# Gathering the first expert's tokens alone, and moving the buffers that its routing uses, in a two-layer flow backbone

## The chip, the cores and the metric

One core of a Trainium2 chip runs the whole program in one launch. The metric is the device time of that core in microseconds (us), from the profiler's clock, as the median over runs.

## What is computed

Two layers. Each layer has a token mixer (four parallel branches, merged and projected by `w_out`) and then a mixture of 16 experts with expert choice: each expert takes its 32 best tokens of a stream. There are two streams of 256 tokens (context and latent); the second layer's experts work on the latent one alone. Cut to what matters here:

```python
def expert_choice_moe(h, router, w1, w3, w2):
    cap = CAPACITY_FACTOR * L // N_EXPERTS                      # 32
    aff = jax.nn.softmax((h @ router).astype(jnp.float32), axis=-1)
    g, idx = lax.top_k(aff.transpose(0, 2, 1), cap)
    xg = jax.vmap(lambda hb, ib: hb[ib])(h, idx)                # (B, 16, 32, 1024)
    a = jnp.einsum('becd,edf->becf', xg, w1)
    b = jnp.einsum('becd,edf->becf', xg, w3)
    y = jnp.einsum('becf,efd->becd', jax.nn.silu(a) * b, w2) * g[..., None]
    return scatter_add(zeros, idx, y)                           # (B, 256, 1024)

def layer(xx):
    xx = xx + mod_x[2] * token_mixer(modulate(xx, norm1_g, ...))
    hx = modulate(xx, norm2_g, mod_x[3], mod_x[4])
    return xx + mod_x[5] * expert_choice_moe(hx, moe_router, moe_w1, moe_w3, moe_w2)
```

All arithmetic is in float32. The weights of the experts are 16 x 3 x 4 MB in each layer.

## The kernel before

SBUF is cut by hand into columns: a base region, a left region (`rb`) and a right region (`rm`, 12288 columns). In a mixer, `rm` holds the hi/lo split of the projections' input; during an MoE, all that is free becomes slots for weights.

**The order of the work.** One program builds all layers, and a scheduling layer orders the instructions of each engine; the code's order is its guide. All weight loads stand in one queue, SP's, which issues in order: a DMA whose slot is still being read holds up those behind it.

**Before an MoE.** `MoePre` (L632 to L674) prepares the routing while the mixer's last projection `w_out` (called `wo` here) runs: the router's weights times the modulation (`AR`), the squares of x (`sq`) and the token sums and logits (`TokenSums`, L573 to L615). It takes the buffer `xt` (x with tokens on partitions) from the end of the base region. `transposes` (L666) fills `xt` by 128x128 transposes on PE and copies on ACT (L674).

**The MoE** (`moe`, L1435). Logits are scaled, softmax runs (exp on ACT at L1454), affinities are transposed, and four rounds of max, max_index and match_replace on DVE (L1468 to L1472) give each expert's 32 tokens; L1473 casts their indices. Then:

- `one_hot(gr)` (L1569) makes the selection matrix `OH` of group `gr` (four experts, 128 columns): a product on DVE (L1571), a broadcast by a matmul with ones, and a comparison with the token numbers on DVE (L1577).
- `gather(gr)` (L1580) multiplies `xt` (the stationary operand, 128x128) by `OH`: 8 chunks k of 128 features, for each stream and each half of the tokens one matmul instruction with 128 moving columns: 32 instructions in the first MoE, 16 in the second. A float32 instruction shows as two records in the trace. The results are scaled and shifted on their way out of PSUM, by ACT (L1605) and DVE (L1603) in turn.
- `weights` (L1607) takes 4 slots of 2048 columns (1 MB each) and issues their DMAs (L1614). An expert has 12 such tiles: 4 of `w1`, 4 of `w3`, 4 of `w2`.
- `ffn(e)` (L1618): 16 instructions for `w1`, 16 for `w3` (PSUM tag `pd`), SiLU on ACT (L1636), a product on DVE (L1637), four transposes (L1640), a copy (L1641), 16 instructions for `w2` (PSUM tag `ps`). A slot is free again when the four instructions that read its tile are through; `use` (L1504) passes it on, and for the first expert gives the first freed ones to buffers that were not there yet.

**The slots' order** (L1484 to L1500): first those of `rb`, then the free ones of the base region, then those of `rm`, last the columns where x itself lay (`xsl`). A slot in `rm` can't be filled before the mixer's last matmul that reads `rm`; one in the base region that covers `AR` and `sq` not before the token logits are done. In the main loop (L1728) group 0 is gathered whole, then the experts run in order; the next group is gathered after the third expert of the one before.

Of the kernel before, what the change touches and what calls it, by code (L numbers as in the profile page):

```python
# [13 lines left out]
AF = mybir.ActivationFunctionType  # L14
OP = mybir.AluOpType
AX = mybir.AxisListType

D = 1024
L = 256
KB = 8  # L20
NE = 16
CAP = 32
# [327 lines left out]
def view(b, off, n):  # L350
    return Buf(b.mem, b.at + off, n)


def build(tc, ins, outT, dbg=None, stop=None):
    nc = tc.nc
    V, A, T, G, S = nc.vector, nc.scalar, nc.tensor, nc.gpsimd, nc.sync
    big = tc.tile_pool(name="big", bufs=1)
    pool = big.__enter__()
    mem = Mem(pool.tile([128, BASE], F32, name="base"), BASE, small=768)
# [17 lines left out]
    def ps(tag):  # L377
        cnt[0] += 1
        return pp.tile([128, 512], F32, name=f"p{tag}{cnt[0]}", tag=tag, bufs=BUFS[tag])
# [9 lines left out]
    mod = [mem.take(96) for _ in range(2)]  # L389
# [4 lines left out]
    ada_raws = [mem.take(512) for _ in range(2)]  # L394
# [14 lines left out]
    def cs(name, off=0, dims=None, **kw):  # L409
        o, c = CN.at[name]  # L410
        if dims is None:
            dims = [[1, kw.pop("n", c - off)]]
        return cn(o + off, dims, **kw)
# [13 lines left out]
    def tr(out, in_):  # L427
        T.transpose(out, in_, ident)  # L428

    def mm(out, lhsT, rhs, start, stop, **kw):  # L430
        return T.matmul(out, lhsT, rhs, start=start, stop=stop, **kw)  # L431
# [141 lines left out]
    class TokenSums:  # L573
# [24 lines left out]
        def tokens(self, mem):  # L598

            W, ns = 512 - self.t0, self.ns  # L600
            out = ps("m")
            part = [mem.take(W) for _ in range(2 if self.AR else 1)]
            V.tensor_copy(part[0](), self.p2[:, 0:W])
            if self.AR:
                A.activation(part[1](n=256), self.pr[:, 0:256], AF.Copy)
            for s in range(ns):
                for tb in range(2):
                    i, c = tb * ns + s, s * 256 + tb * 128
                    mm(out[:, i:i + 1], part[0](c, n=128), cs("one1"), True, True)
            for tb in range(2 if self.AR else 0):  # L610
                mm(out[:, 64 + tb * ns * 16:64 + (tb + 1) * ns * 16], part[1](tb * 128, n=128),
                   cs("ssum" if ns == 1 else "ssum2"), True, True)
            for b in part:
                b.free()
            return out  # L615

    def rs_tokens(p, ns, mem):
# [14 lines left out]
    class MoePre:  # L632


        def __init__(self, l, t0):
            self.l, self.t0 = l, t0
            self.nb = (512 - t0) // 128
            self.ns = self.nb // 2
            self.Ac = mod_cols(l, "g2", 4)
            mem.merge()  # L640
            n = self.nb * D
            self.xt = mem.take_at(mem.end - n, n)
            self.AR = mem.take(512)
            V.tensor_tensor(self.AR(0, [[64, 8], [32, 2], [1, 32]]), sp(l, "router", 0, [[32, 8], [0, 2], [1, 32]]),
                            self.Ac(0, [[2, 8], [1, 2], [0, 32]]), op=OP.mult)
            p = ps("m")
            for k in range(KB):
                mm(p[0:32, 0:2], sp(l, "router", k * 32, n=32), mod[l](3 * 16 + k * 2, n=2), k == 0, k == KB - 1)
            t = mem.take(2)
            V.tensor_copy(t(n=2, np_=32), p[0:32, 0:2])  # L650
            p = ps("m")
            for s in range(2):
                mm(p[:, s * 16:s * 16 + 16], t(s, [[0, 128]], np_=32), cs("ident", n=16, np_=32), True, True)
            t.free()
            self.shr = mem.take(32)
            V.tensor_copy(self.shr(n=32), p[:, 0:32])
            self.sq = [mem.take(512 - t0) for _ in range(4)]
            self.sums = TokenSums(t0, self.sq, self.AR)

        def step(self, k):  # L660
            self.sums.step(k)
            if k == KB - 1:
                for b in self.sq + [self.AR]:
                    b.free()

        def transposes(self):  # L666
            for kh in range(2):
                for i in range(self.nb):
                    p = ps("s")
                    s, tb = divmod(i, 2)  # L670
                    s += 2 - self.ns
                    for q in range(4):
                        tr(p[:, q * 128:q * 128 + 128], xb[0](s * 2048 - xb[1] + (kh * 4 + q) * 256 + tb * 128, n=128))
                    A.activation(self.xt(i * D + kh * 512, n=512), p, AF.Copy)  # L674
# [760 lines left out]
    def moe(l, last, rm, rb, pre, ahead):  # L1435
        t0 = 256 if last else 0
        W = 512 - t0
        NS = 1 if last else 2
        nt = NS * CAP
# [3 lines left out]
        n = nb * 16  # L1443
# [5 lines left out]
                        op=OP.mult)  # L1449
# [8 lines left out]
        ne = NS * 16  # L1458
# [4 lines left out]
        V.tensor_copy(at[0](np_=ne), pa[0:ne, 0:256])  # L1463
        gi = mem.take(64)
        iu = mem.take(32)
        pre.transposes()
        for r in range(4):
            g8, i8, rows = gi(32 + 8 * r, n=8, np_=ne), iu(8 * r, n=8, np_=ne).bitcast(U32), at[r](np_=ne)  # L1468
            V.max(g8, rows)
# [7 lines left out]
        ge = view(raws[2], 512, 256)  # L1477
        OH = view(raws[2], 0, W)
        xg = [view(raws[0], 0, KB * 4 * nt), None]
# [4 lines left out]
        slots = []  # L1484
        for m in (rb, mem, rm):
            m.merge()
            try:
                while True:
                    slots.append(m.take(2048))
            except MemoryError:  # L1490
                pass
            if m is mem:
                late = Buf(mem, cn.at + LATE, 2048)
                slots.append(late)

        x_at, nx = xb[0].at, xb[0].n
        xb[0].free()
# [68 lines left out]
                    else:  # L1566
                        A.activation(dst, src, AF.Copy)

        def one_hot(gr):  # L1569

            V.tensor_tensor(ge(0, [[128, NS], [32, 4], [1, 32]], np_=ne), gi(0, [[0, NS], [0, 4], [1, 32]], np_=ne),  # L1571
                            cs("sel", gr, [[4, NS], [8, 4], [0, 32]], np_=ne), op=OP.mult)
            p = ps("m")
            mm(p[:, 0:NS * 128], cs("ones", np_=ne), ge(n=NS * 128, np_=ne), True, True)
            for s in range(NS):
                for tb in range(2):
                    V.tensor_scalar(OH((s * 2 + tb) * 128, n=128), p[:, s * 128:s * 128 + 128], cs("tok", tb, n=1),  # L1577
                                    rs(8 + tb * NS + s, n=1), op0=OP.is_equal, op1=OP.mult)

        def gather(gr, j0=0, nj=4):  # L1580
            if j0 == 0:
                one_hot(gr)
            x = xg[gr % 2]
            n = nj * 32
            per = min(KB, 512 // (NS * n))
            for k0 in range(0, KB, per):
                p = ps("m")
                ks = range(k0, min(KB, k0 + per))
                for k in ks:
                    for s in range(NS):  # L1590
                        c = ((k - k0) * NS + s) * n
                        for tb in range(2):
                            mm(p[:, c:c + n], pre.xt((s * 2 + tb) * D + k * 128, n=128), OH((s * 2 + tb) * 128 + j0 * 32, n=n),
                               tb == 0, tb == 1)
                for k in ks:
                    for s in range(NS):
                        c = ((k - k0) * NS + s) * n
                        ci = k * 2 + s + 2 - NS
                        src = p[:, c:c + n].rearrange("p (j c) -> p j c", j=nj)
                        dst = x(k * 4 * nt + j0 * nt + s * CAP, [[nt, nj], [1, CAP]])  # L1600
                        A_, sh = pre.Ac(ci, n=1), mod[l](3 * 16 + ci, n=1)
                        if (k + s) % 2:
                            V.tensor_scalar(dst, src, A_, sh, op0=OP.mult, op1=OP.add)  # L1603
                        else:
                            A.activation(dst, src, AF.Identity, bias=sh, scale=A_)  # L1605
# [12 lines left out]
        def ffn(e):  # L1618
            gr, j = divmod(e, 4)
            x = xg[gr % 2]  # L1620
            w1, w3 = weights(0, e), weights(1, e)
            pa, pb = ps("d"), ps("d")
            for p, w in ((pa, w1), (pb, w3)):
                for k in range(KB):
                    for half in range(2):
                        mm(p[half * nt:half * nt + nt, :], x((k * 4 + j) * nt, n=nt),
                           w[k // 2]((k % 2) * 1024 + half * 512, n=512), k == 0, k == KB - 1)
            read = w1 + w3
            n0 = len(slots)
            for b in read[::-1] if e == 0 else read:  # L1630
# [3 lines left out]
            i = e % 2  # L1634
# [3 lines left out]
            p = ps("s")  # L1638
# [4 lines left out]
            if e == NE - 1:  # L1643
                src = ins["moe_w2"][l, e].rearrange("(k p) n -> p k n", p=128)
                c, o, pieces = 0, 2048, []
                for n in LASTW:
                    if o + KB * n > 2048:
                        b, o = slots.pop(0), 0
# [3 lines left out]
                    c, o = c + n, o + KB * n  # L1652
# [72 lines left out]
            S.dma_start(out=cn(LATE + n_, n=CN.n - LATE - n_), in_=ins["cn"][:, LATE + n_:])  # L1725

        nxt, spare = [], []
        gather(0)  # L1728
        for gr in range(4):
            for j in range(4):  # L1730
                ffn(4 * gr + j)
# [49 lines left out]
    for l in range(2):  # L1781
        with phase("right", F32R) as rm:
            if l == 0:
                ada = AdaBack([(0, c) for c in range(2, 5)], mem.take(2048))
            pre, ahead = mixer(l, l == 1, ada, rm, sums)
# [29 lines left out]
```

## Time and profile before

| | |
|---|---|
| runs | 2011.41, 2004.29, 2009.74 us; median 2009.74 |
| profiled execution | 2006.5 us; its span, first to last instruction, 2004.7 us |
| TensorE (PE) busy | 1843.2 us, 92% of the span |
| DVE, ACT, POOL busy | 854.7 (43%), 529.9 (26%), 27.9 (1%) us |
| expert weights | 382 DMAs of 1 MB on SP's queue, median 17 to 18 us from issue to landing |
| other large loads | 152 of 512 KB (`wg`), 96 of 512 KB (`ada_w`, `ada_t`) |

How to read it: PE is the matmul engine and PEld its weight loads, DVE the vector engine, ACT the scalar engine, SPq the queue of SyncE. The first MoE lies at about 645 to 1150 us, the second at about 1535 to 2000 us. A row of a timeline has its start, its length, the engine, the program's line and the operation, output<-input, and in brackets the idle time before and what ended it; "x32" merges 32 records of one kind, so that the length is that of all. A row of windows has, for a stretch, its length, the busy time of each engine (PE, PEld, DVE, ACT, POOL, records in brackets), the clock that PE was granted (1.00 is 2.4 GHz, 0.50 is 1.2 GHz), the DMA engines' share and GB/s.

### The profile page before, as it was taken

Reading aid. Unit: us, or ns where it says so; the run is one execution under the profiler, and the core shown is the slowest. Engines: PE = TensorE matmul, PEld = TensorE weight load, DVE = VectorE, ACT = ScalarE, POOL = GpSimd, SP = SyncE. Lnnn points to the kernel's source line nnn. Section 1 sums busy time; section 2 is a strip of 40 time slices with the busy share of each in tenths; the row PEclk is TensorE's granted clock in tenths of the full one; section 3 lists DMA queues with packets and bytes.
Section 4 is the critical chain, followed back from the end, with each engine's and each line's share of the span. In section 5 each row is a group of like instructions: output and inputs, shape, how many; then the busy total and the mean of one; then the engine's idle time right before and its main releaser. Section 6 shows DMA issues by size and latency. Waiting matters only on the chain.

```text
span 2004.7 us, 28151 instructions
## 1 busy us (share of the span) xinstructions
PE 1843.2 (92%) x11524; PEld 1087.6 (54%) x11524; DVE 854.7 (43%) x1855; ACT 529.9 (26%) x932; POOL 27.9 (1%) x52
## 2 busy tenths in 40 slices
PE   7999999999999899999897799999998999987877
PEld 3667778877887443434232356788997333221213
DVE  5355658798743222221121345869865021110101
ACT  4433447522233110101000243447443000000000
POOL 0000000000000000000000010010000000000000
PEclk9989999999999899999999999999998999999999
DMA  8641122364545999999999855333578999999999
GB/s 312 223 140 58 64 85 78 107 236 136 194 156 218 353 399 350 387 409 409 409 409 409 302 189 180 117 106 137 200 262 336 409 409 409 409 409 409 409 409 332
DMA packets 154148, 550.07 MB, mean 274 GB/s; under 512 B 11042, under 2 KB 22690, under 8 KB 153124
## 3 DMA queue, kind: packets, MB, share of 16 engines
q1 hardware_dynamic: 153444, 545.13, 71.7%
q0 software_dynamic: 576, 3.15, 0.5%
q8 instruction: 91, 1.49, 0.3%
q14 instruction: 37, 0.30, 0.0%
HBM read 545.08 MB, written 3.15 MB: 273 GB/s over the span
## 4 chain that ended last, share of the span: by engine, by line
PE 69%; DMA 19%; DVE 7%; issue 3%; ACT 3%; SPq 0%; DVEq 0%; ACTq 0%
PE pd L431 40%; PE ps L431 15%; DMA base<-moe_w 8%; PE pm L431 7%; DMA r<-moe_w 6%; PE pa L431 4%; DMA base<-ada_w 2%; PE pm L428 1%; DMA base<-wg 1%; DVE base L527 1%; DVE r L844 1%; ACT r L843 1%; PE ps L1640 1%; DMA base<-cb 0%; DVE r L1236 0%
## 5 line engine op out<-in xcount | busy, mean ns | idle before, releaser
L431 PE MATMUL pd<-r 128*128 128x256 f32 (+3 forms) x2976 | 574.4, 364 | 12.9 <-DMA r<-moe_w 6.5
L431 PEld LDWEIGHTS pd<-r 128*128 128x128 f32 (+2 forms) x2976 | 427.3, 184 | 131.4 <-issue 53.8
L431 PE MATMUL pd<-r,r 128*128 128x512 f32 (+3 forms) x1304 | 282.6, 433 | 13.4 <-DMA r<-moe_w 10.8
L431 PEld LDWEIGHTS pd<-r,r 128*128 128x128 f32 (+2 forms) x1304 | 161.8, 166 | 105.0 <-issue 54.8
L844 DVE TENSOR_TENSOR r<-base,r 128x1024 fp32r<-128x1024 f32 x136 | 165.9, 1222 | 110.4 <-ACT r L843 110.0
L843 ACT ACTIVATE r<-base 128x1024 fp32r<-128x1024 f32 x136 | 143.4, 1058 | 252.2 <-PE pd L431 181.2
L431 PE MATMUL ps<-base 32*64 32x64 f32 (+12 forms) x2372 | 177.2, 279 | 15.1 <-DMA base<-hy 5.1
L431 PE MATMUL pd<-r,base 128*32 128x512 f32 (+1 forms) x680 | 166.5, 598 | 11.3 <-DMA r<-moe_w 10.6
L431 PEld LDWEIGHTS ps<-base 32*64 32x64 f32 (+7 forms) x2372 | 112.6, 142 | 76.3 <-issue 42.7
L431 PE MATMUL pm<-base 128*128 128x128 f32 (+12 forms) x660 | 106.1, 327 | 17.5 <-DVE base L1571 5.8
L431 PE MATMUL ps<-r,base 128*64 128x512 f32 (+4 forms) x468 | 98.6, 525 | 12.9 <-DVE base L1641 6.3
L431 PE MATMUL pd<-base 128*32 128x512 f32 (+1 forms) x408 | 100.5, 595 | 6.4 <-DMA base<-moe_w 5.6
L431 PEld LDWEIGHTS pm<-base 128*128 128x128 f32 (+5 forms) x660 | 72.8, 180 | 60.9 <-issue 33.6
L431 PEld LDWEIGHTS pd<-r,base 128*32 128x32 f32 (+1 forms) x680 | 42.0, 122 | 111.2 <-issue 76.4
L1637 DVE TENSOR_TENSOR r<-base,pd 64x512 f32<-64x512 f32 x16 | 10.9, 679 | 214.3 <-PE pd L431 214.3
L1637 DVE TENSOR_TENSOR base<-base,pd 128x512 f32<-128x512 f32 x16 | 11.0, 688 | 190.1 <-PE pd L431 155.9
L1636 ACT ACTIVATE base<-pd 128x512 f32<-128x512 f32 (+1 forms) x32 | 19.0, 594 | 251.1 <-PE pd L431 251.1
L431 PE MATMUL pa<-r,r 128*128 128x512 f32 (+1 forms) x384 | 82.4, 342 | 1.1 <-DVE base L905 1.1
L1687 ACT ACTIVATE base<-ps 32x512 f32<-32x512 f32 (+2 forms) x28 | 14.7, 525 | 251.6 <-PE ps L431 247.2
L1687 ACT ACTIVATE r<-ps 32x512 f32<-32x512 f32 (+2 forms) x32 | 15.3, 480 | 246.2 <-PE ps L431 240.3
L431 PE MATMUL pd<-base,r 128*32 128x512 f32 (+1 forms) x296 | 71.3, 597 | 9.3 <-DMA base<-moe_w 9.3
L1685 DVE COPY r<-ps 32x512 f32<-32x512 f32 (+2 forms) x32 | 17.8, 555 | 123.3 <-ACT r L1687 123.2
(246 smaller groups left out, 1728.8 us busy)
## 6 DMA issues: line engine op xcount, KB each, us to landing
r<-moe_w SPq DMA_DIRECT2D x251, 1024.0 KB, 18.1
base<-moe_w SPq DMA_DIRECT2D x131, 1024.0 KB, 17.4
base<-wg SPq DMA_DIRECT2D x152, 512.0 KB, 3.6
base<-ada_w SPq DMA_DIRECT2D x60, 512.0 KB, 4.7
base<-ada_t SPq DMA_DIRECT2D x24, 512.0 KB, 3.3
r<-ada_w SPq DMA_DIRECT2D x12, 512.0 KB, 10.2
base<-xT SPq DMA_DIRECT2D x4, 1024.0 KB, 6.8
filters<-r SPq DMA_DIRECT2D x8, 256.0 KB, 4.0
```

Source lines behind the costliest of these rows:

```text
L428: T.transpose(out, in_, ident)
L431: return T.matmul(out, lhsT, rhs, start=start, stop=stop, **kw)
L527: V.tensor_tensor_reduce(self.junk() if s == 0 else b(), b(), self.cb(s * 1024, n=1024), 1.0, cs("adab", l * 48 + c * 8 + j, n=1), OP.mult ...
L843: A.activation(w[0](), raw(), AF.Copy)
L844: V.tensor_tensor(w[1](), raw(), F(w[0]()), op=OP.subtract)
L1636: A.activation(s_(np_=rows), pa[0:rows, :], AF.Silu)
L1637: V.tensor_tensor(h_(np_=rows), s_(np_=rows), pb[0:rows, :], op=OP.mult)
L1640: T.transpose(p[:, q * rows:q * rows + rows], h_(q * 128, n=128, np_=rows), cs("ident", n=rows, np_=rows))
L1685: V.tensor_copy(dst, src)
L1687: A.activation(dst, src, AF.Copy)
```

## The change

1. **The first expert's tokens are gathered alone** (`gather_one`): `one_hot` and the matmuls for 32 columns instead of 128, all in one PSUM bank, and four DVE instructions to take it out. The other three experts' tokens are gathered inside `ffn(0)`, between `w1`/`w3` and `w2`, with 96 columns.
2. **A dummy exp** of one column is put on ACT at step 1 of the token sums.
3. **`xt` moves** from the end of the base region to the start of `rm`. `sq` and the sums' parts move to `ada_raws` in part, and `AR` away from the base region's end.
4. **The slots are sorted** by when they come free (`when`): `rb`, free base columns (and, in the second MoE, `rm` from 4096 to 8192), base columns under `AR` and `sq`, the other `rm` slots, and the late one.

```diff
@@ class MoePre
-            n = self.nb * D
-            self.xt = mem.take_at(mem.end - n, n)
-            self.AR = mem.take(512)
+            end = (mem.end - self.nb * D, mem.end)
+            self.AR = mem.take(512, end)
...
-            self.sq = [mem.take(512 - t0) for _ in range(4)]
+            self.sq = [view(ada_raws[i // 2], 256 * (i % 2), 256) if t0 else ada_raws[i] if i < 2 else mem.take(512, end)
+                       for i in range(4)]
+            self.own = [self.AR] if t0 else self.sq[2:] + [self.AR]
...
         def step(self, k):
             self.sums.step(k)
+            if k == 1:
+                z = mem.take(8)
+                A.activation(z(n=1), self.sq[1](0, n=1), AF.Exp, scale=-1.0)
+                z.free()
...
-        def transposes(self):
+        def transposes(self, rm):
+
+            self.xt = rm.take_at(0, self.nb * D)
@@ moe, slots
+        spot = [(b.at, b.at + b.n) for b in pre.own]
+        def when(b):
+            if b is late:
+                return 4
+            if b.mem is rm:
+                return 1 if 2 * KB * W <= b.at < 8192 else 3
+            return 2 if b.mem is mem and any(b.at < o1 and o0 < b.at + 2048 for o0, o1 in spot) else b.mem is mem
+        slots.sort(key=when)
@@ moe, gathers
-        def one_hot(gr):
+        def one_hot(gr, j0, nj):
...
+        def gather_one(gr):
+
+            one_hot(gr, 0, 1)
+            x, p, n = xg[gr % 2], ps("m"), NS * CAP
+            for k in range(KB):
+                for s in range(NS):
+                    c = k * n + s * CAP
+                    for tb in range(2):
+                        mm(p[:, c:c + CAP], pre.xt((s * 2 + tb) * D + k * 128, n=128), OH((s * 2 + tb) * 128, n=CAP),
+                           tb == 0, tb == 1)
+            for k in range(0, KB, 4):
+                dst = x(k * 4 * nt, [[4 * nt, 4], [CAP, NS], [1, CAP]])
+                src = p[:, k * n:(k + 4) * n].rearrange("p (k s c) -> p k s c", s=NS, c=CAP)
+                cols = lambda b, o: b(o + k * 2 + 2 - NS, [[2, 4], [1, NS], [0, CAP]])
+                V.tensor_tensor(dst, src, cols(pre.Ac, 0), op=OP.mult)
+                V.tensor_tensor(dst, dst, cols(mod[l], 48), op=OP.add)
...
         def gather(gr, j0=0, nj=4):
-            if j0 == 0:
-                one_hot(gr)
+            one_hot(gr, j0, nj)
@@ ffn, after the matmuls of w1 and w3
+            if e == 0:
+                gather(0, 1, 3)
@@ main loop
-        gather(0)
+        gather_one(0)
```

The order of the instructions, where the prediction speaks of it. On **PE**, the first MoE's routing to the first expert's `w2`, before (`pm` and `ps` are PSUM tiles; L428 are transposes, `pm` with 128x128 the gather, `pd` the experts' `w1` and `w3`, L1640 the transposes ahead of `w2`, `ps` with 64x512 `w2`):

```order
L431 MATMUL pm_4965<-base 128x256
L431 MATMUL pm_4971<-base 128x128 x8
L431 MATMUL pm_4984<-base 128x128 x8
L431 MATMUL pd_5031<-r_4867,base 64x512
L431 MATMUL pm_4997<-base 128x128 x8
L431 MATMUL pm_5010<-base 128x128 x8
L431 MATMUL pd_5031<-r_4867,base 64x512 x15
L431 MATMUL pd_5032<-r_4867,base 64x512 x8
L431 MATMUL pd_5032<-base 64x512 x8
L431 MATMUL pd_5106<-base 64x512
L1640 MATMUL ps_5067<-base 128x128 x4
L431 MATMUL pd_5106<-base 64x512 x2
```

and in the changed kernel (its L1675 is L1640 before):

```order
L431 MATMUL pm_4966<-base 128x64
L431 MATMUL pm_4972<-base,r_4872 128x32 x32
L431 MATMUL pm_5052<-base 128x192
L431 MATMUL pd_5017<-r_4868,base 64x512 x16
L431 MATMUL pd_5018<-r_4868,base 64x512 x8
L431 MATMUL pd_5018<-base 64x512 x8
L431 MATMUL pm_5058<-base,r_4872 128x96 x8
L431 MATMUL pm_5071<-base,r_4872 128x96 x8
L1675 MATMUL ps_5112<-base 128x128 x3
L431 MATMUL pm_5084<-base,r_4872 128x96 x8
L1675 MATMUL ps_5112<-base 128x128
L431 MATMUL pm_5097<-base,r_4872 128x96 x8
```

One gather of 32 instructions has become two: 32 narrow ones ahead of `w1`, and 32 of 96 columns ahead of the first `w2` (`ps_5122`, 16 instructions, which follows). The second MoE has the same with 16 and 16.

On **SP**, the first MoE's first tiles, before (`r_4867` is `rb`, `r_4871` is `rm`; `r_4867` x6 in the last row is the first reuse):

```order
L1614 DMA r_4867<-moe_w 128x2x1024 x2
L1614 DMA base<-moe_w 128x2x1024
L1614 DMA r_4871<-moe_w 128x2x1024
L1614 DMA base<-moe_w 128x2x1024 x2
L1614 DMA r_4871<-moe_w 128x2x1024 x5
L1614 DMA base<-moe_w 128x2x1024 x2
L1614 DMA r_4867<-moe_w 128x2x1024 x6
```

and in the changed kernel (its L1647 is L1614 before, `r_4868` is `rb`, `r_4872` is `rm`):

```order
L1647 DMA r_4868<-moe_w 128x2x1024 x2
L1647 DMA base<-moe_w 128x2x1024 x4
L1647 DMA r_4872<-moe_w 128x2x1024
L1647 DMA base<-moe_w 128x2x1024
L1647 DMA r_4872<-moe_w 128x2x1024 x3
L1647 DMA base<-moe_w 128x2x1024 x2
L1647 DMA r_4868<-moe_w 128x2x1024 x6
```

Three more tiles of the base region stand ahead of the first tile of `rm`, and two fewer are in `rm`. From the first row on, it is 13 tiles until the first reuse in both.

## Rows read from the trace of the kernel before

**Rows 1.** Page of before, part 2: GB/s in 40 slices of 50.1 us.
```profile
GB/s 312 223 140 58 64 85 78 107 236 136 194 156 218 353 399 350 387 409 409 409 409 409 302 189 180 117 106 137 200 262 336 409 409 409 409 409 409 409 409 332
```
**Rows 2.** Windows (us, busy times, granted clock, DMA share, GB/s), first MoE's start.
```profile
660.00:665.00 5.00, 4.49 (x20) 4.16 (x20) 1.69 (x5) 0.28 (x1) 0.00 (x0) 0.50 1.03 409
665.00:670.00 5.00, 5.00 (x36) 4.07 (x35) 1.46 (x4) 1.59 (x5) 0.00 (x0) 0.94 0.89 356
670.00:675.00 5.00, 5.00 (x32) 2.72 (x32) 1.46 (x4) 3.08 (x5) 0.00 (x0) 1.00 0.10 16
```
**Rows 3.** DMA issues on SP, first MoE: two reuses (start us, us, engine, line).
```profile
673.60 0.37 SPq L1614 DMA_DIRECT2D r<-moe_w  x1
689.86 0.37 SPq L1614 DMA_DIRECT2D base<-moe_w  x1
```
**Rows 4.** One DMA into an empty queue (KB, us from issue to landing), issue at 642.19.
```profile
r<-moe_w SPq DMA_DIRECT2D x1, 1024.0 KB, 4.7
```
**Rows 5.** Waits of PE (total us, times, longest us), 690 to 977 us.
```profile
PE ps L1640 <- DVE base L1637: 5.1, 7, 0.9
```
**Rows 6.** Waits of PE, 977 to 1121 us (end of the first MoE).
```profile
PE pd L431 <- DMA r<-moe_w: 9.7, 14, 2.0
```
**Rows 7.** Timeline of ACT, first MoE's routing.
```profile
650.28 1.28 ACT L1454 ACT_TABLE_LOAD   x1
651.58 0.26 ACT L1454 ACTIVATE base<-base 128x64 f32<-128x64 f32 x1
```
**Rows 8.** Timeline of DVE, first MoE's one-hot.
```profile
658.66 0.41 DVE L1571 TENSOR_TENSOR base<-base 32x256 f32<-32x256 f32 x1
660.38 1.37 DVE L1577 TENSOR_SCALAR base<-pm,base 128x128 f32<-128x128 f32 x4 [1.31 <-PE pm L431]
```
**Rows 9.** Timeline of PE, first MoE: one-hot, gather, first expert.
```profile
660.85 6.09 PE L431 MATMUL pm<-base 128*128 128x128 f32 x32 [0.51 <-DVE base L1577]
667.87 3.84 PE L431 MATMUL pm<-base 128*128 128x128 f32 x32
671.64 3.65 PE L431 MATMUL pd<-r,base 128*64 128x512 f32 x16
687.92 4.46 PE L431 MATMUL ps<-base 128*64 128x512 f32 x20
```
**Rows 10.** Timeline of PEld (weight loads), the same gather.
```profile
660.85 5.90 PEld L431 LDWEIGHTS pm<-base 128*128 128x128 f32 x32 [1.23 <-DVE base L1577]
667.87 3.65 PEld L431 LDWEIGHTS pm<-base 128*128 128x128 f32 x32 [0.81 <-ACT base L1605]
```
**Rows 11.** Timeline of PE, matmuls with one moving column, full clock.
```profile
645.76 1.45 PE L431 MATMUL pm<-base 128*128 128x1 f32 x12
```
**Rows 12.** Timeline of DVE, two pieces of the gather's evacuation.
```profile
670.46 0.73 DVE L1603 TENSOR_SCALAR base<-pm,base 128x128 f32<-128x128 f32 x2 [2.26 <-ACT base L1605]
```
**Rows 13.** DMA issues on SP, second MoE: first after `wo`, two reuses.
```profile
1534.18 0.37 SPq L1614 DMA_DIRECT2D base<-moe_w  x1
1553.26 0.37 SPq L1614 DMA_DIRECT2D base<-moe_w  x1
1569.39 0.37 SPq L1614 DMA_DIRECT2D r<-moe_w  x1
```
**Rows 14.** The DMA issued at 1553.26: us from issue to landing, behind a queue.
```profile
base<-moe_w SPq DMA_DIRECT2D x1, 1024.0 KB, 7.5
```
**Rows 15.** Timeline of PE, second MoE: `wo`'s end, gather, experts 0 and on.
```profile
1528.79 1.72 PE L431 MATMUL pd<-r 128*128 128x256 f32 x13
1545.62 5.75 PE L431 MATMUL pm<-base 128*128 128x128 f32 x32 [0.51 <-DVE base L1577]
1551.31 8.78 PE L431 MATMUL pd<-base 128*32 128x512 f32 x40
1567.45 2.74 PE L431 MATMUL ps<-r 128*32 128x512 f32 x12
```
**Rows 16.** Windows by engine, the second mixer after its first projections.
```profile
1180.00:1500.00 320.00, 308.78 (x2775) 266.61 (x2774) 226.35 (x533) 154.11 (x287) 14.03 (x28) 1.00 0.48 167
```

More of the change, by code (lines that the diff above doesn't have):

```diff
@@ L601, in tokens @@
             out = ps("m")
-            part = [mem.take(W) for _ in range(2 if self.AR else 1)]
+            part = [view(b, 0, W) for b in ada_raws] if self.AR else [mem.take(W)]
             V.tensor_copy(part[0](), self.p2[:, 0:W])
@@ L612, in tokens @@
                    cs("ssum" if ns == 1 else "ssum2"), True, True)
-            for b in part:
-                b.free()
+            if not self.AR:
+                part[0].free()
             return out
@@ L661, in step @@
             self.sums.step(k)
+            if k == 1:
+                z = mem.take(8)
+                A.activation(z(n=1), self.sq[1](0, n=1), AF.Exp, scale=-1.0)
+                z.free()
             if k == KB - 1:
-                for b in self.sq + [self.AR]:
+                for b in self.own:
                     b.free()
-        def transposes(self):
+        def transposes(self, rm):
+            self.xt = rm.take_at(0, self.nb * D)
             for kh in range(2):
@@ L1465, in moe @@
         iu = mem.take(32)
-        pre.transposes()
+        pre.transposes(rm)
         for r in range(4):
@@ L1567, in restore_x @@
                         A.activation(dst, src, AF.Copy)
-        def one_hot(gr):
-            V.tensor_tensor(ge(0, [[128, NS], [32, 4], [1, 32]], np_=ne), gi(0, [[0, NS], [0, 4], [1, 32]], np_=ne),
-                            cs("sel", gr, [[4, NS], [8, 4], [0, 32]], np_=ne), op=OP.mult)
+        def one_hot(gr, j0, nj):
+            n = nj * 32
+            V.tensor_tensor(ge(0, [[n, NS], [32, nj], [1, 32]], np_=ne), gi(0, [[0, NS], [0, nj], [1, 32]], np_=ne),
+                            cs("sel", j0 * 8 + gr, [[4, NS], [8, nj], [0, 32]], np_=ne), op=OP.mult)
             p = ps("m")
-            mm(p[:, 0:NS * 128], cs("ones", np_=ne), ge(n=NS * 128, np_=ne), True, True)
+            mm(p[:, 0:NS * n], cs("ones", np_=ne), ge(n=NS * n, np_=ne), True, True)
             for s in range(NS):
                 for tb in range(2):
-                    V.tensor_scalar(OH((s * 2 + tb) * 128, n=128), p[:, s * 128:s * 128 + 128], cs("tok", tb, n=1),
+                    V.tensor_scalar(OH((s * 2 + tb) * 128 + j0 * 32, n=n), p[:, s * n:s * n + n], cs("tok", tb, n=1),
                                     rs(8 + tb * NS + s, n=1), op0=OP.is_equal, op1=OP.mult)
+        def gather_one(gr):
[13 more added lines that the diff above has]
+                V.tensor_tensor(dst, dst, cols(mod[l], 48), op=OP.add)
         def gather(gr, j0=0, nj=4):
-            if j0 == 0:
-                one_hot(gr)
+            one_hot(gr, j0, nj)
             x = xg[gr % 2]
```

## The prediction

> **What bounds the kernel now.** I read the page's slices first, then the windows of the two stretches in which an MoE starts, then PE's waits, and last the timelines of SP, PE, DVE and ACT there. The slices show 409 GB/s in slices 17 to 21 and 31 to 38 [rows 1]: there weights stream without a pause. At that rate a tile of 1 MB takes 1.049 MB / 409 GB/s = 2.56 us; into an empty queue it lands 4.7 us after its issue [rows 4].
>
> *First MoE.* By SP's order 21 tiles fit before a slot is used twice. They have landed by about 670 us, and in 670 to 675 us only 16 GB/s move [rows 2]: the queue is dry until the first expert's first four `w1` instructions free a slot at 673.60; the slots that `w2` frees follow from 689.86 on [rows 3]. From 690 to 977 us PE waits for DVE and ACT alone, never for a weight; the 7 waits ahead of the transposes cost 0.7 us each [rows 5]. From 977 us on it waits for tile after tile [rows 6]. So PE sets the pace first, and as SP's issues hang on PE's reads, a delay of PE before 830 us moves the stream that ends the MoE by as much. Three tiles landing earlier before 645 us help nobody here: the number of tiles before the first reuse is the same.
>
> *Second MoE.* The stream begins with the issue at 1534.18 [rows 13] and runs at 409 GB/s to the end [rows 1], so each us by which it runs earlier, without a later gap, counts.
>
> **The change, part by part.** The sum is made against the profiled execution, 2006.5 us, which stands 3.2 us under the median shown (2009.74).
>
> *Early exp.* The table load takes 1.28 us right ahead of exp [rows 7]. The dummy moves it into `wo`'s stretch, where ACT has idle time. Some 0.2 us of it lay beside the end of exp's input, so I take -1.1 us (bounds 0 and -1.3). The SiLU's table load is behind exp in both kernels.
>
> *One-hot.* From its product to the first gather record 2.19 us pass (658.66 to 660.85), with 0.41 us for the product and 1.37 / 4 = 0.34 us for a comparison [rows 8, 9]. A quarter of the columns shortens all three steps; the fixed part of each isn't shown. I take -0.9 us (bounds 0 and -1.4).
>
> *`gather_one`, first MoE.* It starts at 660.85 - 2.0 = 658.85. It has 64 records, as many as the old gather, only narrower. The old ones took 6.09 / 32 = 0.19 us at clock 0.50 and 3.84 / 32 = 0.12 us at full clock [rows 2, 9], and a record with one moving column also takes 1.45 / 12 = 0.12 us [rows 11]: at full clock width costs nothing below 128 columns. At half clock I have no narrow record; bounds are 0.12 and 0.24 us, and I take 0.19, since the weight loads themselves stood 5.90 / 32 = 0.18 us apart there and 3.65 / 32 = 0.11 us after [rows 10]. The clock came back 0.6 us into 665 to 670 us (mean 0.94) [rows 2], 4.7 us after the gather's start; I take the same here, 24 records: 24 x 0.19 + 40 x 0.12 = 9.4 us, to 668.2. Then, behind the last matmul, a DVE product and the first sum: by 0.37 us for a piece of 128x128 [rows 12], 0.85 us, so `w1` begins at 669.05. Before, it ran from 671.64, with one instruction (0.43 us) done earlier [rows 9], so from 671.2. Gain: **-2.2 us**, and the first reuse at 673.60 comes earlier by as much.
>
> The Trainium skill (page "TensorE: Matmul & The Clock Gate", section "LDWEIGHTS (loading the stationary operand)") gives a weight load as its columns divided by 1.2 in ns, 107 ns for 128 columns, and makes no difference by the clock. By it the 64 narrow records would take 6.8 us instead of 9.4, the first MoE would lose 2.5 us less and the second 2.1 us less, and the sum below would be +1.2 instead of +5.8. The row at half clock, 0.18 us per load, speaks against it.
>
> *The other three experts' gather, first MoE.* 32 instructions more, 64 records of 96 columns at full clock: 64 x 0.117 = +7.5 us of PE, all between `w3` and `w2`. Its cover is one of the idle waits ahead of the transposes, 0.7 to 0.9 us [rows 5]: -0.8. So `w2`, from 687.92 before [rows 9], and with it the slots it frees from 689.86 on, come later by 7.5 - 0.8 - 2.2 = **+4.5 us**. Queued behind these slots on SP are all later tiles, and nothing of PE's work is removed elsewhere: the lag lasts to 977 us and passes into the stream. Bounds: +1.5 (narrow records at 0.12 us throughout, one-hot at its best) and +8 (half clock throughout, no gain from exp).
>
> *Slots, second MoE.* By SP's order 22 tiles are loaded before the first reuse in both; 15 instead of 14 are issued before `wo` ends, and the first after it goes to `rm`, which waits for `wo`'s last matmul at 1528.79 + 1.72 = 1530.5 [rows 15] instead of the token logits. It is issued 3.7 us before the 1534.18 of today, and one tile fewer stands behind it. But the 22 tiles then end the earlier: the next slot, freed by `w1` at 1553.26, took 7.5 us to land behind a queue, to 1560.8 [rows 13, 14]; without one it lands at 1558.2, -2.6 us. There is no exp load to save here. The narrow gather has 32 records: from 1545.1, 24 x 0.19 + 8 x 0.12 = 5.5 us, with evacuation `w1` starts at 1551.5, against 1551.31 [rows 15]. The wide one adds 32 x 0.117 = 3.7 us, less 0.6 us of idle, so `w2` starts 3.3 us later than 1567.45 [rows 15], and the slot that it freed at 1569.39 [rows 13] is free at 1572.7. The tile in it lands at 1572.7 + 4.7 = 1577.4; before, six tiles behind 1560.8, at 1576.1. A gap opens that the earlier start can't close: **+1.3 us**, to the end of the kernel. Bounds: -3 (the gate at `w2` doesn't bind) and +3.
>
> *The second mixer.* Experts' last tiles lie in other regions, so `rm` and the scan's matmuls come in another order there. From 1180 to 1500 us PE is busy 308.8 of 320 us [rows 16]: at most 11.2 us can be gained, and the order alone doesn't say which way. I take 0, with -3 and +11 as bounds.
>
> *Other edits.* `sq`, `AR` and the sums' parts in other places and the sort itself cost nothing: same instructions, beside `wo`'s matmuls.
>
> Sum: 4.5 + 1.3 + 0 = +5.8, so 2012.3 for an execution like the profiled one, 2015.5 on the median's footing. Between the two I forecast **2014 us**, a difference of 0.2%. About 0.5% (10 us) is what a measurement of this kernel can tell from no change, so the class is "no difference".
>
> **The rivals.**
> - *The earlier starts decide.* If the slots that `w1` frees carry the stream over `w2`'s delay, the first MoE keeps -2.2 and the second gains 2.6: 2014 - 5.8 - 4.8 = 2003 us. For it: the dry queue at 670 to 675 us and the 7.5 us of queue [rows 2, 14]. Against it: from 690 us on PE itself is the pace, and it has more to do. Chance 0.2.
> - *The clock stays low.* If narrow matmuls don't bring the clock back from 0.50 while `gather_one` runs, 40 records cost 0.07 us more, +2.8, and 8 in the second MoE, +0.6: 2017 us. For it: PE is idle ahead of the gather in both. Against it: the old gather got the clock back within itself. Chance 0.1. The Trainium skill (same page, "Why this matters for your kernels") warns that thin matmuls let the clock swing; the trace of before has no long run of such narrow ones at that place to show it.
> - *Slower.* In the second mixer the scan's matmuls, moved ahead of projections, wait for DVE without cover. It decides once PE's idle time in a stretch like 1180 to 1500 us, now 11.2 us [rows 16], grows by 6 us or more; doubled, the kernel takes 2014 + 11 = 2025 us. For it: the moved order; against it: most projections still stand beside the scans. Chance 0.1.
> - *The change doesn't do what it says.* If the tokens of the first expert come no earlier (the one-hot's fixed parts and the evacuation eat the gain) and the later gather fills waits more than I think, nothing moves: 2010 us. Chance 0.15.
>
> **How the numbers follow.** My forecast has 0.45. Faster by over 0.5%, below 1999.7 us, is a third to a half of the first rival: 0.09. Slower, above 2019.8, is over half of the third, and tails of the second and of the bounds: 0.10. The rest, 0.81, lies within 0.5%. The range reaches from 2001 us (most of the first rival) to 2021 us (upper bounds of the first MoE); outside are the ends of the first and third rival.
>
> **What would show it.** Right: in the first MoE a narrow gather of 64 records in about 9.4 us, `w1` some 2 us earlier, `w2` some 4 us later than 687.9, a dry queue of 5 us or more before `w2`'s first slot, and the MoE's last tile 4 us later; in the second MoE the first tile after `wo` issued near 1530.5 on the old footing, and a short gap in the stream near 1573. Wrong: `w2` of the first expert earlier than before, no gap behind the tiles that `w1`'s slots bring, a gather at clock 0.50 to its end, or PE's idle time in the second mixer changed by more than 3 us.

## The result, and the profile after

The changed kernel takes **2025.28 us** (median of 4 runs, 2021.65 to 2029.5) against 2007.01 us of the kernel before on the same chip (4 runs, 2000.78 to 2011.41): a ratio of **1.0084**, 95% interval 1.0059 to 1.0110. The medians are 18.3 us apart, and the ratio stands for 17 us (12 to 22): the change is slower. I had forecast no difference, and the time lies above my range. The profiled execution of the changed kernel has a span of 2019.6 us, 14.9 us over that of before.

In the page of the changed kernel the slices show the same picture as [rows 1], with 409 GB/s in the same slices of the first MoE and from one slice later on in the second:

```profile
GB/s 309 219 154 55 64 78 79 138 237 125 188 188 301 211 390 389 400 409 409 409 409 409 260 164 190 115 85 157 199 275 319 361 409 409 409 409 409 409 409 332
```

The first MoE tells most. These are the first copy of the transposes on ACT (a fixed point at the end of `wo`), and then PE's one-hot, narrow gather, `w1` with `w3`'s first half, the first half of the other experts' gather, and `w2`; they answer to [rows 9]:

```profile
639.80 0.60 ACT L681 ACTIVATE r<-ps 128x512 f32<-128x512 f32 x1 [0.88 <-PE ps L428]
651.87 0.68 PE L431 MATMUL pm<-base 32*128 32x64 f32 x2 [5.64 <-DVE base L1588]
652.96 13.86 PE L431 MATMUL pm<-base,r 128*128 128x32 f32 x64 [0.40 <-DVE base L1594]
668.00 12.30 PE L431 MATMUL pd<-r,base 128*64 128x512 f32 x48 [0.24 <-DVE base L1612]
683.66 3.81 PE L431 MATMUL pm<-base,r 128*128 128x96 f32 x32
692.56 7.09 PE L431 MATMUL ps<-base 128*64 128x512 f32 x32
```

The narrow gather took 13.86 us for 64 records, 0.217 us each, where I had 9.4 us. The windows (as in [rows 2]: length, busy times, granted clock, DMA share, GB/s) show why:

```profile
655.00:660.00 5.00, 5.00 (x25) 5.00 (x25) 0.00 (x0) 0.00 (x0) 0.00 (x0) 0.50 0.27 102
660.00:665.00 5.00, 5.00 (x25) 5.00 (x25) 0.00 (x0) 0.00 (x0) 0.00 (x0) 0.50 0.00 0
665.00:670.00 5.00, 4.76 (x17) 2.94 (x18) 2.89 (x9) 0.00 (x0) 0.00 (x0) 0.50 0.00 0
670.00:675.00 5.00, 5.00 (x22) 1.46 (x20) 0.00 (x0) 0.00 (x0) 0.00 (x0) 0.84 0.41 132
```

PE was busy without a pause, and its clock stayed at 0.50 (1.2 GHz) through the whole gather and into `w1`; `w1`, with the full clock in 670 to 675 us for part of the time, took 12.30 us for 48 records (0.256 us each, against 10.09 / 45 = 0.224 before, shown below). From 660 to 670 us no weight moved. SP's two reuses answer to [rows 3]:

```profile
671.72 0.37 SPq L1647 DMA_DIRECT2D r<-moe_w  x1
694.54 0.37 SPq L1647 DMA_DIRECT2D base<-moe_w  x1
```

ACT's first copy and `w1` in the first MoE before, and ACT's first copy in the second MoE, before and in the change:

```profile
645.52 0.60 ACT L674 ACTIVATE base<-ps 128x512 f32<-128x512 f32 x1 [1.06 <-PE ps L428]
671.64 10.09 PE L431 MATMUL pd<-r,base 128*64 128x512 f32 x45
1533.04 0.60 ACT L674 ACTIVATE base<-ps 128x512 f32<-128x512 f32 x1 [0.92 <-PE ps L428]
1540.24 0.60 ACT L681 ACTIVATE r<-ps 128x512 f32<-128x512 f32 x1 [0.83 <-PE ps L428]
```

From ACT's first copy to `w2` it was 692.56 - 639.80 = **52.8 us**. Before, that copy began at 645.52 and `w2` at 687.92 [rows 9]: 42.4 us. So `w2` came 10.4 us later (I had 4.5).

The second MoE, PE's narrow gather, `w1` and `w3`, second gather, `w2` (against [rows 15]), and two windows:

```profile
1552.67 7.03 PE L431 MATMUL pm<-base,r 128*128 128x32 f32 x32 [0.41 <-DVE base L1594]
1560.48 11.46 PE L431 MATMUL pd<-base 128*32 128x512 f32 x40
1577.02 3.81 PE L431 MATMUL pm<-base,r 128*128 128x96 f32 x32
1582.04 0.62 PE L431 MATMUL ps<-r 128*32 128x512 f32 x1
```

```profile
1560.00:1565.00 5.00, 4.89 (x14) 1.23 (x15) 1.39 (x7) 0.00 (x0) 0.00 (x0) 0.50 0.00 0
1565.00:1570.00 5.00, 5.00 (x22) 1.20 (x20) 0.00 (x0) 0.00 (x0) 0.00 (x0) 0.91 0.98 328
```

Again 0.22 us a record, the clock at 0.50 until `w1` had run for some 5 us, 11.46 instead of 8.78 us for the same 40 records, and `w2` 41.8 us after ACT's first copy (1540.24) instead of 34.4: +7.4 us (I had 3.3). SP's issues answer to [rows 13]. Counted from ACT's first copy, the first tile behind `wo` is issued 3.6 us earlier than before, and the tile that waits for `w1`, issued at 1564.15, 3.7 us later:

```profile
1537.74 0.37 SPq L1647 DMA_DIRECT2D r<-moe_w  x1
1564.15 0.37 SPq L1647 DMA_DIRECT2D base<-moe_w  x1
1584.82 0.37 SPq L1647 DMA_DIRECT2D r<-moe_w  x1
```

10.4 + 7.4 = 17.8 us, about the loss. Whether it is the same time, the experiments have to show.

### The profile page after: what moved, and what is told of

Same layout as the page of the kernel before. It is cut to its first block, busy times and chain, and to the rows that moved or that the text cites. A ratio compares the mean times of both kernels' runs of the same rounds, so it can differ in the third digit from the quotient of the medians.

```text
span 2019.6 us, 28375 instructions
## 1 busy us (share of the span) xinstructions
PE 1862.7 (92%) x11624; PEld 1103.9 (55%) x11624; DVE 858.4 (43%) x1871; ACT 530.7 (26%) x934; POOL 26.4 (1%) x52
## 4 chain that ended last, share of the span: by engine, by line
PE 70%; DMA 18%; DVE 7%; ACT 2%; issue 2%; SPq 1%; DVEq 0%; ACTq 0%
PE pd L431 41%; PE ps L431 15%; DMA r<-moe_w 9%; PE pm L431 7%; PE pa L431 5%; DMA base<-moe_w 5%; DMA base<-ada_w 2%; PE pm L428 2%; DMA base<-wg 1%; DVE r L851 1%; DVE base L527 1%; ACT r L850 1%; PE ps L1675 1%; DMA base<-xT 0%; SPq L1647 0%
## 5 line engine op out<-in xcount | busy, mean ns | idle before, releaser
L431 PE MATMUL pd<-r,r 128*128 128x512 f32 (+3 forms) x1224 | 265.9, 423 | 12.3 <-DMA r<-moe_w 8.8
L431 PE MATMUL ps<-base 32*64 32x64 f32 (+11 forms) x2532 | 193.0, 283 | 13.9 <-DMA base<-hy 4.3
L431 PEld LDWEIGHTS ps<-base 32*64 32x64 f32 (+7 forms) x2532 | 120.7, 142 | 86.0 <-issue 51.9
L431 PE MATMUL pd<-r,base 128*32 128x512 f32 (+1 forms) x576 | 142.4, 605 | 9.6 <-DMA r<-moe_w 8.1
L431 PE MATMUL pd<-base 128*64 128x512 f32 (+1 forms) x512 | 128.4, 607 | 7.7 <-DMA base<-moe_w 6.9
L431 PE MATMUL pd<-base,r 128*32 128x512 f32 (+1 forms) x376 | 88.9, 596 | 9.8 <-DMA base<-moe_w 9.8
L431 PE MATMUL ps<-r,base 128*64 128x512 f32 (+2 forms) x308 | 79.6, 597 | 12.0 <-ACT r L753 5.4
L431 PEld LDWEIGHTS pm<-base,r 128*128 128x128 f32 x512 | 71.3, 218 | 30.9 <-issue 16.4
L431 PEld LDWEIGHTS pd<-r,base 128*32 128x32 f32 (+1 forms) x576 | 35.4, 122 | 95.2 <-issue 64.5
L431 PE MATMUL pm<-base,r 128*128 128x128 f32 (+3 forms) x512 | 80.6, 312 | 3.2 <-DVE base L1594 1.8
L431 PEld LDWEIGHTS pd<-base 128*64 128x64 f32 (+1 forms) x512 | 34.6, 127 | 85.9 <-issue 65.7
```

## The experiments

Two theories. **A**: the loss is in the gather of the first expert alone: the narrow gather at half clock, and the PE work that a second gather adds. **B**: it is in the order that moved buffers and sorted slots give to the streams and the second mixer. The column of `w2` in this table is its start less that of ACT's first copy of the transposes, from each run's profile, as worked out above; "kept busy" are runs with matmuls that nobody reads ahead of the gather. The ratios are to the kernel before on the same chip.

| kernel | ratio (95% interval) | `w2`, first MoE | second MoE |
|---|---|---|---|
| before | 1 | 42.4 us | 34.4 us |
| changed | 1.0084 (1.0059 to 1.0110) | 52.8 | 41.8 |
| whole gather | 0.9988 (0.9971 to 1.0004) | 41.1 | 34.8 |
| gather alone | 1.0085 (1.0066 to 1.0104) | 54.1 | 40.4 |
| kept busy, narrow | 1.0114 (1.0092 to 1.0135) | 55.4 | 42.1 |
| kept busy, whole (13) | 1.0011 (0.9994 to 1.0028) | 43.6 | 35.9 |
| kept busy, whole (14) | 1.0003 (0.9990 to 1.0017) | 44.7 | 36.9 |
| two experts first | 1.0077 (1.0052 to 1.0102) | 53.2 | 40.6 |
| rest behind `w2` | 1.0079 (1.0057 to 1.0101) | 46.3 | 39.1 |
| kept busy, whole (7 and 8) | 0.9967 (0.9946 to 0.9989) | 39.3 | 32.3 |
| before, kept busy | 0.9993 (0.9972 to 1.0014) | 40.4 | 32.3 |
| extra gather | 1.0031 (1.0014 to 1.0048) | 48.2 | 36.9 |

### Undo the gather alone, and do it alone

```diff
 (changed kernel, whole gather)
-        gather_one(0)
+        gather(0)
...
-            if e == 0:
-                gather(0, 1, 3)
```

> The changed kernel with the old gather: group 0 gathered whole (128 columns) before the first expert, nothing gathered inside it; early exp, moved buffers and sorted slots stay. Theory A (the narrow gather keeps the clock at 0.50, and that is the loss): the clock is back within the gather as before, first expert's w2 about 2 us earlier than before after wo's end, time 2 us under before, -6 to +2. Theory B (the loss is in the order that slots and buffers give the second mixer and the streams): some 8 us over before remain.

```diff
 (kernel before, gather alone: gather_one and one_hot as in the change)
-        gather(0)
+        gather_one(0)
...
+            if e == 0:
+                gather(0, 1, 3)
```

> The kernel before with the first expert's gather alone and the others' inside the first expert, and nothing else of the change. Theory A: all of the loss is here, 15 to 20 us over before, gather_one at 0.21 to 0.22 us a record and clock 0.50 until the first expert's w1 runs, in both MoEs. Theory B: half of it or less, 5 to 9 us.

With the whole gather back, PE's gather (first half), `w1` and `w2` in the first MoE are as in [rows 9], 1.3 us earlier after the copies:

```profile
659.67 6.14 PE L431 MATMUL pm<-base,r 128*128 128x128 f32 x32 [0.51 <-DVE base L1594]
670.52 10.08 PE L431 MATMUL pd<-r,base 128*64 128x512 f32 x45
686.80 7.04 PE L431 MATMUL ps<-base 128*64 128x512 f32 x32
```

In the kernel before with the gather alone, the gather (its 64 records, and two more that the view merges with them), `w1` and `w2`:

```profile
649.81 14.79 PE L431 MATMUL pm<-base 128*128 128x32 f32 x66 [0.41 <-DVE base L1578]
664.85 12.47 PE L431 MATMUL pd<-r,base 128*64 128x512 f32 x48 [0.25 <-DVE base L1596]
689.58 7.09 PE L431 MATMUL ps<-base 128*64 128x512 f32 x32
```

The first is not told from before (0.9988), the second is as slow as the whole change (1.0085). To within the intervals (some 4 us each way) all of the loss is in the gather alone; theory B falls as its cause.

### The work that the second gather adds, by itself

```diff
 (kernel before)
+            if e == 0:
+                for k0 in range(0, KB, 4 // NS):
+                    p = ps("m")
+                    for i in range(8):
+                        c = (i // 2) % (2 * NS) * 96 if NS == 2 else (i // 2) * 96
+                        mm(p[:, c:c + 96], pre.xt(...), OH(..., n=96), i % 2 == 0, i % 2 == 1)
             read = w1 + w3
```

> The kernel before, its whole gather kept, with 32 matmuls of 96 columns (16 in the second MoE) added inside the first expert between w3 and w2, whose result nobody reads: the work that the second gather adds, at full clock, without a narrow gather. Theory A (the loss of 18 us has two parts, the second gather's added PE work at full clock and the low clock of the narrow one): 64 and 32 records at 0.12 us less the idle time they fill, +6.7 and +3.1 us, so 9 to 10 us over before (0.5%); w2 6 to 7 us and 3 us later after the transposes. Rival (the added work hides in waits, and the low clock alone makes the 18 us): 0 to 4 us over before.

The added matmuls, 7.39 us for 64 records, and `w2`:

```profile
678.35 7.39 PE L431 MATMUL pm<-base 128*128 128x96 f32 x64
686.96 7.08 PE L431 MATMUL ps<-base 128*64 128x512 f32 x32
```

`w2` came 5.8 and 2.5 us later than before, near what I had worked out. So of the 10.4 and 7.4 us of the change, the added work makes 5.8 and 2.5. The other 4.6 and 4.9 I put down to the slow clock; this is a difference and not a run, since none had the narrow gather at full clock to its end, and in the first MoE the early exp and the shorter one-hot, some 2 us, are already taken off. In time it was 0.31% (6 us), under the 9 to 10 expected; in this run's trace the stretch from `w2` to the second mixer was 5 us shorter than before, with a shorter wait, told below. The rival, that the added work hides, falls; its upper end of 4 us lies inside the interval of 2.8 to 9.6 us, but `w2` is moved in both MoEs.

### Keep PE busy up to the gather

```diff
 (changed kernel; below, with the whole gather: 13, 14, then 7 and 8 of them)
         pre.transposes(rm)
+        pw = ps("d")
+        for i in range(13):
+            mm(pw, pre.xt((nb - 1) * D + 512, n=128), pre.xt((nb - 1) * D + 512, n=512), True, True)
```

> The changed kernel with 13 matmuls of 512 columns, whose result nobody reads, on PE between the transposes of x and the one-hot, in both MoEs, to fill its idle time during the choice of tokens. Theory A: the clock stays 1.00 up to the narrow gather; if narrow matmuls only fail to raise the clock, its records take 0.12 us (7.7 us instead of 13.9 in the first MoE, 3.9 instead of 7.0 in the second), and w1 runs at full clock: about 4 us over before. If narrow matmuls let the clock fall again, most of the 18 us stays. Theory B: 10 us or more over before.

The added matmuls behind the affinities' transposes, and the narrow gather:

```profile
652.28 10.46 PE L431 MATMUL pd<-r 128*128 128x512 f32 x24
663.51 11.27 PE L431 MATMUL pm<-base,r 128*128 128x32 f32 x64 [0.40 <-DVE base L1597]
```

The clock around the narrow gather, which began at 663.51:

```profile
662.00:664.00 2.00, 1.60 (x9) 0.78 (x7) 0.85 (x4) 0.00 (x0) 0.00 (x0) 1.00 0.06 23
664.00:666.00 2.00, 2.00 (x21) 2.00 (x20) 0.36 (x2) 0.00 (x0) 0.00 (x0) 1.00 0.00 0
666.00:668.00 2.00, 2.00 (x14) 2.00 (x13) 0.00 (x0) 0.00 (x0) 0.00 (x0) 0.60 0.00 0
668.00:670.00 2.00, 2.00 (x11) 2.00 (x11) 0.00 (x0) 0.00 (x0) 0.00 (x0) 0.50 0.00 0
```

The clock was at 1.00 when the narrow gather began, and **fell to 0.50 within it**, some 3 us after its start, with PE busy without a pause from 664 to 674 us; it was still at 0.50 when `w1` began. So the narrow gather does not only fail to raise the clock; behind a busy PE it lets it fall. Behind the same 13 matmuls the whole gather kept 1.00 (next run), so the 0.4 us of idle time ahead of the gather, 0.5 us there, is not what made it fall. The run was no faster than the change, because the 13 matmuls took 0.87 us each, twice the 0.43 us of one of an expert's, and held up the one-hot by 5.2 and 3.5 us.

> The changed kernel with the old whole gather, as in the run with the whole gather, and with the same 13 matmuls that nobody reads. Theory A: the old gather, too, paid for the low clock (32 records at 0.19 instead of 0.12 us and the one-hot's matmul), so 2 to 4 us per MoE under the run with the whole gather: 5 to 9 us under before. Theory B: no gain over the run with the whole gather.

> The changed kernel with the old whole gather, and with 14 matmuls of 64x512, whose result nobody reads, on PE between the transposes of x and the one-hot: half as long each as those of the runs before (0.43 us an instruction), so that they end before the one-hot's matmul could start, 6.2 us after the transposes of the affinities. Theory A (the low clock at the MoEs' start is a price by itself): the gathers run at 0.12 us a record from the first, w1 some 2.5 us earlier than in the run with the whole gather in each MoE, time 4 to 5 us under that run, so about 7 us under before (-12 to -2). Rival: the streams of weights take the gain back, no more than 2 us under that run.

Both misses: with the whole gather the clock stayed at 1.00 and the gather's first 32 records took 4.1 us instead of 6.1, but the added matmuls ran too long in both. Halving their stationary columns (64 instead of 128) did not shorten them: still 0.87 us. So I put fewer:

> As the run with 14 matmuls that nobody reads, with 7 in the first MoE and 8 in the second: in the two runs before each took 0.87 us, and the one-hot came 5 to 6 us and 3.4 to 4.4 us too late behind them. With whole gather, early exp, moved buffers and sorted slots. Theory A (what the low clock costs at an MoE's start comes back in full when PE is kept busy): the first expert's w2 2.5 us earlier after the transposes than in the run with the whole gather (38.6 instead of 41.1 us) and 2.2 us in the second (32.5 instead of 34.8), time 4 to 5 us under that run: 0.3 to 0.4% under before. Rival (the streams take it back): as the run with the whole gather, 0.1% under before.

> The kernel before with the same 7 and 8 matmuls that nobody reads and nothing of the change. Theory A: each gather's first 32 records at 0.12 us, w1 and w2 some 2.5 and 2.2 us earlier after the transposes, about 4 to 5 us under before (0.2%). Rival: same as before.

With 7 and 8 (changed kernel, whole gather): the added matmuls, the gather's two halves, and the clock:

```profile
649.95 5.36 PE L431 MATMUL pd<-r 128*64 128x512 f32 x12
657.05 4.13 PE L431 MATMUL pm<-base,r 128*128 128x128 f32 x32 [0.50 <-DVE base L1597]
662.11 3.84 PE L431 MATMUL pm<-base,r 128*128 128x128 f32 x32
```

```profile
650.00:655.00 5.00, 5.00 (x13) 1.51 (x12) 4.78 (x19) 0.00 (x0) 0.00 (x0) 1.00 1.01 401
655.00:660.00 5.00, 3.95 (x26) 3.17 (x26) 2.50 (x9) 0.46 (x1) 0.00 (x0) 1.00 0.90 358
```

`w2` came 1.8 and 2.5 us earlier than with the whole gather alone, and 3.1 and 2.1 us earlier than before. The time is **0.33% under before** (0.11 to 0.54%): this version beats both kernels. Its interval overlaps that of the whole gather alone (0.9971 to 1.0004), so the traces show the earlier `w2`, but the runs don't resolve what the added matmuls give in time. On the kernel before the same matmuls moved `w2` 2.0 and 2.1 us; the time (0.9993) is not told from no change, nor from the 4 us expected.

### Twice the width, and another place for the rest

```diff
 (changed kernel, two experts first)
-        gather_one(0)
+        gather(0, 0, 2)
...
-                gather(0, 1, 3)
+                gather(0, 2, 2)
```

> The changed kernel with two experts' tokens (64 columns) gathered ahead of w1, and the other two's (64 columns) inside the first expert: the same number of instructions at the same places as in the changed kernel, twice as wide ahead of w1. Theory A (what counts is whether the matmuls are wide enough to bring the clock back): if 64 columns bring it back as 128 did, some 5 us after the gather's start, w2 comes 4 us (first MoE) and 3 us (second MoE) later than before and the time is 7 to 8 us over before; if not, 15 to 18 us over before with records of 0.21 us or more at clock 0.50. Theory B (the second gather's place and work make the loss whatever the clock): 15 to 18 us over before, with the clock back.

The gather of 64 columns, and the clock:

```profile
656.19 13.91 PE L431 MATMUL pm<-base,r 128*128 128x64 f32 x64 [0.44 <-DVE base L1594]
```

```profile
660.00:665.00 5.00, 5.00 (x26) 5.00 (x25) 0.60 (x2) 1.02 (x3) 0.00 (x0) 0.50 0.01 2
665.00:670.00 5.00, 5.00 (x24) 4.91 (x24) 0.60 (x2) 0.09 (x1) 0.00 (x0) 0.50 0.00 0
```

13.91 us for 64 records, as long as with 32 columns, at 0.50 to its end: at half clock these records take 0.217 us with 32 columns and with 64, against 0.12 at full clock. The time is that of theory A's second case.

```diff
 (changed kernel, rest behind w2)
-            if e == 0:
-                gather(0, 1, 3)
...
             for b in w2:
                 use(b, e)
+            if e == 0:
+                gather(0, 1, 3)
```

> The changed kernel with the gather of the other three experts behind the first expert's w2 in the program instead of ahead of it; the narrow gather stays. Theory A (PE's added time is what passes to the end, wherever it stands): 14 to 18 us over before. Rival (the slots that w2 frees late make the loss): w2 7 us and 4 us earlier than in the changed kernel, and the time about 11 us under the changed kernel, 7 us over before.

`w2` came 6.5 and 2.7 us earlier than in the change, and in the first MoE the first slot that it frees 6.5 us, and the time stayed (1.0079). The edit did this in part only: in the trace 20 of the 64 records of the rest, and 18 of 32 in the second MoE, still ran ahead of `w2`. What passes to the end is PE's added time, not the late slots: theory A.

## Why the prediction was wrong

**The step that failed** is that of `gather_one`: "4.7 us after the gather's start; I take the same here, 24 records", said of the clock's return. That took the clock's return from the old gather, whose records were wider, as a matter of time alone. In the change it did not return within the gather at all, nor in the first microseconds of `w1`. In the first MoE two terms follow from it: all 64 records at 0.217 us instead of 24 at 0.19 and 40 at 0.12, 13.9 instead of 9.4 us (+4.5); and `w1` at half clock for some 3.5 us, 48 records at 0.256 instead of 0.224 (+1.5). In the second: 7.0 instead of 5.5 us (+1.5) and `w1` with 11.46 instead of 8.78 us (+2.7). Together 10.2 us; with them the forecast's +5.8 would have been +16.0. A second, smaller step failed with them: of the 3.3 us by which I had `w2` late in the second MoE, I let +1.3 reach the end. From that `w2` to the end of the span it took 2004.7 - 1567.45 = 437.2 us before and 2019.6 - 1582.04 = 437.6 in the change, so a lag of `w2` passed whole. That adds 2.0 and makes +18.0, near the 17 to 18 measured.

**The rival that came true** was "the clock stays low", to which I gave 0.1 and 2017 us. Its mechanism was right and its price was too small, on two counts: I priced a slow record at 0.19 us, which was the mean of the old gather, 0.217 records and 0.12 ones together, and let the slow clock end with the gather, leaving `w1` out. The trace of before had the right price in its first 4.15 us, 19 records at clock 0.50 (0.218 us each, with 128 columns):

```profile
660.85:665.00 4.15, 4.15 (x19) 4.15 (x20) 1.22 (x4) 0.28 (x1) 0.00 (x0) 0.50 1.02 406
```

**The weight loads.** The Trainium skill (page "TensorE: Matmul & The Clock Gate", section "LDWEIGHTS (loading the stationary operand)") would have the 64 narrow records at 6.8 us, an estimate from its rule of the columns divided by 1.2 (107 ns). The trace has 13.9: at half clock each took 0.217 us, at full clock 0.12, so the figure comes near at full clock alone. The Trainium skill's row on thin matmuls (same page, section "Why this matters for your kernels") warns of a swinging clock where a loop waits for DMAs between its tiles. The run that entered the narrow gather at 1.00 saw the clock fall, as in the warning, but no wait for a DMA stood there.

**Right.** The early exp: from ACT's first copy to the one-hot's product on DVE 11.8 us instead of 13.1, -1.3 (I had -1.1). The one-hot: from there to the gather 1.4 instead of 2.2 us, -0.8 (I had -0.9). Its product in the change, against [rows 8]:

```profile
651.60 0.21 DVE L1588 TENSOR_TENSOR base<-base 32x64 f32<-32x64 f32 x1
```

The first tile behind the second `wo`, issued 3.6 us earlier (I had 3.7). The second gather's added work: 7.4 us of records for my 7.5, `w2` +5.8 and +2.5 us by itself (I had +6.7 and +3.1). That a lag of `w2` is one of PE and passes to the end wherever the gather stands (rest behind `w2`). That the earlier starts of the streams bring nothing: the whole-gather run has them all and is not told from before.

**The second mixer.** I took 0, with up to +11. From SP's issue of the last piece of the last expert's `w2` to ACT's first copy of the next MoE it took 410.7 us before, and 418.9 in the change; in the whole-gather run 416.3, and 416.1 in the gather-alone run, which has the old buffers. PE's waits, change, 1160 to 1200 us, and the clock behind them:

```profile
PE ps L431 <- ACT base L969: 2.0, 1, 2.0
PE pd L431 <- ACT r L850: 1.8, 1, 1.8
```

```profile
1180.00:1200.00 20.00, 16.16 (x121) 13.37 (x114) 3.81 (x5) 7.95 (x11) 0.00 (x0) 0.83 0.48 157
```

A scan matmul and a projection wait there for ACT without cover, and the clock dips to 0.83: the third rival's mechanism, with ACT in DVE's place. These two waits stand in the traces of all eight kernels with the change's buffers and slots, and in none of the four with the old ones. How much of the 8.2 us they make isn't shown: the gather-alone run is 5.4 us longer than before without them. Against it stands a wait in the first MoE, before only (PE's waits in 738 to 815 us, and the clock in a window behind the wait):

```profile
PE ps L431 <- DVE base L1641: 3.1, 2, 2.7
```

```profile
770.00:780.00 10.00, 10.00 (x35) 2.94 (x32) 0.23 (x1) 0.58 (x1) 0.00 (x0) 0.76 1.00 377
```

In the change this wait is 0.3 us long and the clock does not fall: from the issue of tile 48 to that of tile 72 it takes 64.5 us instead of 72.7. The two side effects nearly cancel: the whole-gather run has both and is not told from before, the gather-alone run has neither these waits nor the shorter one and is as slow as the change. The extra-gather run has the old buffers and the shorter wait too, 0.9 us, so that one is a matter of the order that the scheduler finds, and not of the buffers alone; no run tests either by itself.

## What to carry to other kernels

Price a group of matmuls behind an idle stretch at the clock at which it will run to its end, and those behind it too: a narrower group can keep the engine at half clock longer and cost more than the wide one it replaces. Splitting one gather into two costs a full second set of records when a record's price doesn't fall with its width. Where PE must wait for other engines, matmuls whose result nobody reads can keep its clock up (what they gain in time by themselves was not clear of the noise here), but count their length from a row of the same shape, so that they end before the work they prepare.

## What was not expected of the hardware

- The clock fell from 1.00 to 0.50 while PE was busy without a pause by the profile: 64 records of 32 moving columns, each 0.12 us at first and 0.2 us after.
- A matmul instruction of 64x512 took 0.87 us when it ran alone (26 records in 11.37 us, run with 14), and 0.43 us as one of an expert's: there, the two halves of an expert's output are written by alternate instructions to different partitions. That the halves overlap is my reading; no run tests it.
- The clock dips at places where the two kernels' code does not differ. In the profiled execution of before, 100 to 120 us, and in that of the change:

```profile
100.00:120.00 20.00, 18.75 (x99) 11.26 (x97) 4.99 (x8) 5.89 (x9) 0.00 (x0) 0.83 0.49 162
```

```profile
100.00:120.00 20.00, 19.95 (x175) 11.71 (x177) 6.70 (x11) 7.71 (x13) 0.00 (x0) 1.00 0.59 191
```

The diff touches nothing that runs there. Between 93 and 105 us PE waited for loads of `ada_w` three times before, 0.6, 1.4 and 1.3 us, and twice in the change, 0.2 and 1.7 us; the change has its dip, to 0.83 too, in 120 to 130 us. The change's trace reached the first MoE 5.7 us earlier than that of before; what makes such dips is open. So one pair of traces doesn't give the sum to a few us, and the medians do.
